# In-projection weights on another DMA queue, a table built in two steps, and gate weights issued after other tiles

## The chip, the cores and the metric

The kernel runs on one core of one Trainium2 chip. The metric is device time in microseconds (us), from the start of the launch on the core to its end; three runs of the kernel before gave 1465.84, 1471.44 and 1471.6 us.

## The reference

One layer of a hybrid decoder for 2048 positions and 1024 channels, all in float32. Cut to its steps:

```
h  = rmsnorm(x, norm_w)
u, zs, q, k, v, za = split(h @ w_in)             # 1024 -> 6 x 512 columns
ya = s5(u)                                       # 32 groups of 16 channels, complex state of 64,
                                                 #   scan over positions, gelu, half-GLU
ya = ya * silu(zs)
yb = differential_attention(rope(rmsnorm(q)), rope(rmsnorm(k)), v)   # 4 heads, two causal
                                                 #   softmax maps each, w1 - lambda * w2
yb = rmsnorm(yb) * 0.8 * silu(za)
x1 = x + concat(ya, yb) @ w_out                  # 1024 -> 1024
out = x1 + sigmoid(x1 @ w_gate) * (p @ w_proj)   # w_gate 1024 x 1024, w_proj 256 x 1024
```

## The kernel before

Every product is made from three TensorE products of rounded halves (high x high, high x low, low x high), so each operand exists as a pair: a cast on ScalarE (ACT) makes the high half, a subtraction on VectorE (DVE) or GpSimd (POOL) the low half. The program is written as Python generators, and a scheduler of the framework simulates a timeline and puts the instructions of each engine in one fixed order; each engine then runs its own list strictly in that order, DMA starts included. DMAs are started by SyncE (SP), a few by ACT.

**In-projection (0 to about 684 us).** It runs over 12 blocks, each 512 columns of `w_in` for one half of the positions, in the order u, u, k, zs, v, q, za, zs, k, v, q, za. A block has 8 weight chunks of 128 x 512. `build_w` (L276) makes one chunk: raw values into one of three `wraw` buffers (L279), `wh` on ACT (L282), `wl` on DVE (L283); `wh` and `wl` have 8 slots, one block's worth. So at the change from one block to the next the first three chunks already lie in `wraw`; their casts wait until the last tile of the old block has read the slots, and the raw loads of chunks 3 to 7 each wait until a `wl` has freed a `wraw` buffer. TensorE's products are at L757 (first block), L778 (u and zs) and L824 (q, k, v, za).

Between them runs the generator `ssm()`: for each quad of four channel groups `four()` (L546) builds parameter tables, among them the rotation table of each pair of groups (two products and a sum on DVE, L581 to L585) which goes out to `tab_scr` (L586) and comes back per group as `tab` (L599). `tx`, the tile that leaves, has one buffer, so the second pair's table waits until the first one has been stored. Then per group two products (L530), a rotation, a scan and a rotation back (L633 to L644).

**Attention (684 to about 1140 us).** Four heads, with the first half of the out-projection (L928) as filler.

**Second half of the out-projection (1140 to about 1235 us).** Eight tiles t of 256 positions. Tiles 0 to 2 (`EOP = 3`) run through a single PSUM tile `pmf`: each of their eight pieces is added to `x1` on DVE (L1185), and the next piece starts when that add is done. Tiles from 3 on use seven banks `pm3`, with one add for two pieces (L1189).

Beside it `gate_w()` (L1139) prepares the gate weights as seven sums of quadrants, four rounds k of two units each. A round loads two `wgr` tiles (two buffers in all, so a round's loads wait for the readers of the round before), gated by a one-column copy of the last finished `x1` (L1160, POOL); the units then make casts on ACT (L1149), differences (L1154) and low halves (L1150) on DVE and POOL. `GWS` says how many units are issued after which tile t, so it sets which `x1` a round's loads wait for: the one of the tile before.

**Gate product and per-layer input (1250 us to the end).** The operands are cast by ACT (`oph`, L1235); their pool lies where the `wgr`, `wgt` and `yin` buffers were, so the first cast waits for the last reader of those. L1262 is the gate product, L1278 the projection of p.

Of the kernel before, what the change touches and what calls it, by code (L numbers as in the profile page):

```python
# [11 lines left out]
F32 = mybir.dt.float32  # L12
# [3 lines left out]
ALU = mybir.AluOpType  # L16
# [49 lines left out]
WB = 8  # L66
ACB = 3
EOP = 3
GWS = {3: 2, 4: 2, 5: 3, 6: 1}
XEB = 14  # L70
RA3 = 2
SSE = 0
# [46 lines left out]
def hymba_kernel(ctx, tc, x_t, p_t, positions, norm_w, w_in, lam_re, lam_im, log_dt, b_re, b_im,  # L119
                 c_re, c_im, ssm_d, glu_w, glu_b, q_norm_w, k_norm_w, lq1, lk1, lq2, lk2,  # L120
                 subln_w, w_out, w_proj, w_gate, out):
    nc = tc.nc
    V, A, G, T = nc.vector, nc.scalar, nc.gpsimd, nc.tensor
    UE = (G, V)[SSE]
    win = w_in[0]
# [10 lines left out]
    tab_scr = [tc.dram_tile([128, 2, 17, 16], F32, name=f"tab_scr{i}") for i in range(16)]  # L136
# [61 lines left out]
    with ExitStack() as p1:  # L198
# [77 lines left out]
        def build_w(c0, k):  # L276
            def make():
                raw = pr.tile([128, 512], F32, name="wraw", bufs=WRB)
                nc.sync.dma_start(raw, win[k * 128:(k + 1) * 128, c0:c0 + 512])  # L279
                wh = pw.tile([128, 512], F32R, name="wh")  # L280
                wl = pw.tile([128, 512], F32R, name="wl")
                A.activation(wh, raw, AF.Copy, scale=nw[:, k:k + 1])  # L282
                V.scalar_tensor_tensor(wl, raw, nw[:, k:k + 1], wh.bitcast(F32), op0=ALU.mult, op1=ALU.subtract)  # L283
                return wh, wl
            return make
# [27 lines left out]
        def ssm():  # L313
# [55 lines left out]
            with tc.tile_pool(name="ssA", bufs=1) as sp:  # L369
                t32 = {}  # L370

                def nt(nm, shape=(128, NG)):
                    t32[nm] = sp.tile(list(shape), F32, name="s_" + nm)
                    return t32[nm]
# [7 lines left out]
                t1 = nt("t1")  # L382
# [38 lines left out]
                k = 1  # L421
# [8 lines left out]
                nr, den, t1 = nt("nr"), nt("den"), nt("t2")  # L430
# [46 lines left out]
                for (Tt, n_) in ((Tb, 16), (Ta, 16)):  # L477
                    V.memset(Tt[0][:, :, 0:1], 1.0)
                    V.memset(Tt[1][:, :, 0:1], 0.0)
                    k = 1  # L480
# [31 lines left out]
            with tc.tile_pool(name="ssB", bufs=2) as sp:  # L512
# [3 lines left out]
                def split(x_, nm, cols):  # L516

                    hi = sp.tile([128, cols], F32R, name=nm + "h", bufs=SPB[nm])
                    lo = sp.tile([128, cols], F32R, name=nm + "l", bufs=SPB[nm])
                    h_, l_ = hi, lo  # L520
                    if len(x_.shape) > 2:
                        g_, k_, p_ = x_.shape[1:]
                        h_, l_ = (t_.rearrange("q (g l p) -> q g l p", g=g_, l=k_) for t_ in (hi, lo))
                    A.copy(h_, x_)
                    V.tensor_tensor(l_, x_, h_.bitcast(F32), op=ALU.subtract)
                    return hi, lo
# [7 lines left out]
                def spread(par4, o_, l0):  # L534

                    r_ = sp.tile(sh, F32, name="na", bufs=1)
                    t_ = sp.tile([128, 2, 17, 16], F32, name="tabt", bufs=1).rearrange("q s a b -> q (s a b)")[:, :512]
                    t_ = t_.rearrange("q (g l p) -> q g l p", g=4, l=L)
                    V.tensor_tensor(r_, par4[:, :, o_:o_ + 16].unsqueeze(2).to_broadcast(sh),
                                    par4[:, :, 65 + l0:73 + l0].unsqueeze(3).to_broadcast(sh), op=ALU.mult)  # L540
                    V.tensor_tensor(t_, par4[:, :, o_ + 16:o_ + 32].unsqueeze(2).to_broadcast(sh),
                                    par4[:, :, 74 + l0:82 + l0].unsqueeze(3).to_broadcast(sh), op=ALU.mult)
                    V.tensor_tensor(r_, r_, t_, op=ALU.add)
                    return r_

                def four(q4, out_):  # L546


                    par4 = sp.tile([128, 4, NPAR], F32, name="parg")
                    nc.sync.dma_start(par4, par_scr[q4])  # L550
                    pt2 = sp.tile([128, 2, NTAB], F32, name="pt2", bufs=1)
                    nc.sync.dma_start(pt2, ptab_scr[q4])
                    na = spread(par4, 0, 1)

                    dd = sp.tile([128, 4, GP], F32, name="dd")
                    nc.sync.dma_start(dd.rearrange("q g p -> q (g p)"), ssm_d[0, q4 * 64:q4 * 64 + 64].partition_broadcast(128))
                    G.affine_select(out=dd, in_=dd, pattern=[[0, 4], [-1, GP]], compare_op=ALU.is_equal,
                                    fill=0.0, base=-112, channel_multiplier=1)
                    yield
                    pr_ = ps_ss.tile([128, 512], F32, name="pss")  # L560
                    for g in range(4):
                        T.matmul(pr_[:, g * 16:g * 16 + 16], lhsT=na[:, g].rearrange("q l p -> q (l p)"),
                                 rhs=par4[:, g, 32:48], start=True, stop=True)
                    rs = sp.tile([128, 64], F32, name="rs", bufs=1)
                    V.tensor_tensor(rs, pr_[:, :64], dd.rearrange("q g p -> q (g p)"), op=ALU.add)
                    nc.sync.dma_start(r_scr[q4][0:128, :], rs)
                    M = sp.tile([128, L, 64], F32, name="M", bufs=1)

                    r0 = r_scr[q4][0:128, :]
                    nc.sync.dma_start(M, bass.AP(tensor=r0.tensor, offset=r0.offset, ap=[[64, 128], [GP * 64, L], [1, 64]]))  # L570
                    pw_ = ps_ss.tile([128, 512], F32, name="pss")
                    for g in range(4):
                        T.transpose(pw_[:, g * 128:g * 128 + 128], na[:, g].rearrange("q l p -> q (l p)"), ident)
                    wa = split(pw_, "wa", 512)
                    yield

                    sht = [128, 2, 17, 16]
                    for e in range(2):
                        tx = sp.tile(sht, F32, name="tx", bufs=1)
                        t1 = sp.tile(sht, F32, name="tabt", bufs=1)  # L580
                        V.tensor_tensor(tx, pt2[:, e, 0:17].unsqueeze(1).unsqueeze(3).to_broadcast(sht),  # L581
                                        pt2[:, e, 34:66].rearrange("q (s b) -> q s b", s=2).unsqueeze(2).to_broadcast(sht), op=ALU.mult)
                        V.tensor_tensor(t1, pt2[:, e, 17:34].unsqueeze(1).unsqueeze(3).to_broadcast(sht),
                                        pt2[:, e, 66:98].rearrange("q (s b) -> q s b", s=2).unsqueeze(2).to_broadcast(sht), op=ALU.mult)
                        V.tensor_tensor(tx, tx, t1, op=ALU.add)  # L585
                        nc.sync.dma_start(tab_scr[q4 * 2 + e], tx)  # L586
                    yield
                    wc = spread(par4, 32, 0)
                    out_[q4] = par4, wa, M, wc
                    yield  # L590
# [15 lines left out]
                for _ in four(0, made):  # L606
                    pass
# [4 lines left out]
                for g in range(NG):  # L612
                    gl = g % 4
                    gs = slice(gl * 128, gl * 128 + 128)
                    if gl == 0:
                        par4, wa4, _, wc_raw = made.pop(g // 4)
                        parts = four(g // 4 + 1, made) if g < NG - 4 else iter(())
# [48 lines left out]
            with tc.tile_pool(name="ssC", bufs=1) as pg:  # L666
# [5 lines left out]
                for k in range(4):  # L672
                    for e in range(2):
                        raw = pg.tile([128, 256], F32, name="gg", bufs=GLB)
# [5 lines left out]
                for cq in range(8):  # L680
                    while ("zs", cq // 4) not in written:
                        yield
                    c0 = cq * 32
# [250 lines left out]
    with ExitStack() as p2:  # L934
# [90 lines left out]
        for h in range(H):  # L1025
# [6 lines left out]
            for i in ORD[h]:  # L1032
# [6 lines left out]
                for qt in range(2):  # L1039
# [16 lines left out]
                    c0 = 0  # L1056
# [67 lines left out]
    with ExitStack() as p3:  # L1124
# [12 lines left out]
        with ExitStack() as p3a:  # L1137
# [38 lines left out]
            for t, i in enumerate(order):  # L1176
# [15 lines left out]
                else:  # L1192
                    kept.append(x1)
                for _ in range(GWS.get(t, 0)):
                    next(gw)
# [200 lines left out]
```

## Time and profile before

| | |
|---|---|
| three runs | 1465.84, 1471.44, 1471.6 us (median 1471.44) |
| profiled execution | 1468.54 us, of it the span of the profile 1466.8 us |
| TensorE (PE) busy | 1389.2 us, 95% of the span |
| DVE, ACT, POOL busy | 73%, 52%, 36% |
| mean granted TensorE clock | 0.982 of full speed |

TensorE is busy nearly all the time, so a change can shorten the span by what TensorE waits (some 78 us in the whole program) and by the stretches that it runs at the lower clock behind a wait. Where it waits, and for whom, is in the rows further down. "[4.66 <-X]" behind a row says that the engine sat idle 4.66 us before it and that X ended the wait.

### The profile page before, as it was taken

To read this page: it belongs to the slowest core of one execution; us is meant where nothing else is said; L and a number is where in the kernel's file an instruction comes from. 1 tells how busy PE (TensorE), PEld (TensorE's weight loads), DVE (VectorE), ACT (ScalarE), POOL (GpSimd) and SP (SyncE) were. 2 spreads that over 40 slices of the span, in tenths; PEclk is the share of its full clock that TensorE was granted. 3 is DMA by queue.
4 is the path that set the end of the run, shared out by engine and by line. 5 is a ranking of instruction groups with operands and counts; after the bars stand their busy time and mean duration, and the time that the engine had idled before them with its cause. 6 is when DMAs were issued, how large, how long until landed. Compare 5 with 4: busy or idle time off the path is not lost.

```text
span 1466.8 us, 27419 instructions
## 1 busy us (share of the span) xinstructions
PE 1389.2 (95%) x9602; PEld 1279.5 (87%) x9602; DVE 1067.0 (73%) x2527; ACT 768.0 (52%) x1689; POOL 522.4 (36%) x670
## 2 busy tenths in 40 slices
PE   7999899999899999999899999999999996999998
PEld 7998798778698878888699999988989896899998
DVE  8568788789898866774687767767887248656754
ACT  8543335456554545553577677777787213332231
POOL 6632410043010411340255455544335334543440
PEclk9999899999999999999999999999999998899999
DMA  7448666546755287556854644644443455132221
GB/s 244 131 127 263 200 190 210 159 125 211 237 179 177 94 232 185 150 168 203 255 145 125 181 127 119 177 127 152 116 144 122 153 189 205 58 116 76 70 80 58
DMA packets 219410, 230.34 MB, mean 157 GB/s; under 512 B 62712, under 2 KB 168328, under 8 KB 216712
## 3 DMA queue, kind: packets, MB, share of 16 engines
q1 hardware_dynamic: 216968, 224.40, 49.8%
q10 hardware_dynamic: 2304, 4.20, 0.8%
q8 instruction: 75, 1.23, 0.3%
q14 instruction: 63, 0.52, 0.1%
HBM read 152.19 MB, written 84.72 MB: 162 GB/s over the span
## 4 chain that ended last, share of the span: by engine, by line
PE 48%; DVE 19%; DMA 15%; ACT 6%; issue 6%; POOL 5%; SPq 2%; ACTq 0%; DVEq 0%; POOLq 0%
PE pg L1262 11%; PE pmf L928 7%; PE po L1099 7%; PE pss L1063 7%; PE ptw L1095 3%; PE pl L1278 3%; DMA wraw<-in_w_in_dram 3%; PE pmm L824 2%; PE pss L707 2%; PE pmm L778 2%; POOL qst L846 2%; DMA tab_scr<-tx 2%; DVE wl L283 2%; PE pm L928 2%; DVE zz L644 1%
## 5 line engine op out<-in xcount | busy, mean ns | idle before, releaser
L824 PE MATMUL pmm<-wh,xh 128*128 128x512 f32 x512 | 197.6, 395 | 7.0 <-ACT wh L282 6.6
L824 PE MATMUL pmm<-wl,xh 128*128 128x512 f32 x512 | 200.8, 395 | 2.1 <-DVE wl L283 2.1
L824 PE MATMUL pmm<-wh,xl 128*128 128x512 f32 x512 | 200.2, 393 | 0.0
L1063 PE MATMUL pss<-ks,qd 128*128 128x512 f32 (+3 forms) x640 | 185.1, 387 | 7.5 <-DVE st L1065 4.0
L1074 ACT ACTIVATE s<-s,st 128x1024 f32<-128x1024 f32 (+4 forms) x192 | 171.5, 897 | 37.3 <-DVE st L1065 32.8
L1262 PE MATMUL pg<-oph,wg 128*128 128x256 f32 x896 | 164.1, 286 | 15.4 <-ACT oph L1235 15.4
L1262 PEld LDWEIGHTS pg<-oph,wg 128*128 128x128 f32 x896 | 141.6, 195 | 15.6 <-ACT oph L1235 15.6
L1099 PE MATMUL po<-vt,wt 128*128 128x128 f32 x1088 | 152.3, 276 | 2.9 <-ACT yo L1111 1.5
L1099 PEld LDWEIGHTS po<-vt,wt 128*128 128x128 f32 x1088 | 142.2, 192 | 11.2 <-ACT wt L1097 3.2
L1065 DVE CUSTOM_DVE_ANT_0 s<-pss,mk,st 128x512 f32<-128x512 f32 (+2 forms) x192 | 122.1, 651 | 23.3 <-PE pss L1063 21.7
L778 PE MATMUL pmm<-xh,wl 128*128 128x256 f32 x448 | 128.9, 291 | 4.1 <-DVE wl L283 4.1
L778 PE MATMUL pmm<-xh,wh 128*128 128x256 f32 x448 | 124.9, 294 | 6.0 <-DVE stg L788 3.2
L778 PE MATMUL pmm<-xl,wh 128*128 128x256 f32 x448 | 128.5, 290 | 0.0
L1262 PE MATMUL pg<-opl,wg 128*128 128x256 f32 x448 | 127.2, 285 | 0.3 <-POOL opl L1236 0.3
L824 PEld LDWEIGHTS pmm<-wh,xh 128*128 128x128 f32 x512 | 96.2, 189 | 27.6 <-ACT wh L282 8.7
L1063 PEld LDWEIGHTS pss<-ks,qd 128*128 128x128 f32 x640 | 100.8, 192 | 17.5 <-DVE st L1065 8.0
L824 PEld LDWEIGHTS pmm<-wl,xh 128*128 128x128 f32 x512 | 96.6, 189 | 21.1 <-DVE wl L283 3.0
L824 PEld LDWEIGHTS pmm<-wh,xl 128*128 128x128 f32 x512 | 96.7, 189 | 18.2
L928 PE MATMUL pmf<-yh,woh 128*128 128x256 f32 x352 | 105.0, 298 | 4.5 <-DVE x L1185 3.6
L596 POOL TENSOR_TENSOR U<-U,rl 128x256 f32<-128x256 f32 x32 | 28.3, 884 | 220.5 <-DMA U<-ug_scr 169.5
L1065 DVE CUSTOM_DVE_ANT_0 s<-pss,mk 128x512 f32<-128x512 f32 (+3 forms) x128 | 78.5, 629 | 31.2 <-PE pss L1063 26.7
L928 PE MATMUL pmf<-yl,woh 128*128 128x256 f32 x352 | 99.8, 284 | 0.0
(385 smaller groups left out, 3906.1 us busy)
## 6 DMA issues: line engine op xcount, KB each, us to landing
wraw<-in_w_in_dram SPq DMA_DIRECT2D x96, 256.0 KB
xraw<-in_x_t_dram SPq DMA_DIRECT2D x40, 256.0 KB
tab<-tab_scr SPq DMA_DIRECT2D x64, 136.0 KB
qd<-qh_scr SPq DMA_DIRECT2D x64, 128.0 KB
qd<-ql_scr SPq DMA_DIRECT2D x64, 128.0 KB
xr<-in_x_t_dram SPq DMA_DIRECT2D x32, 256.0 KB
yin<-yt_scr SPq DMA_DIRECT2D x16, 512.0 KB
xp_scr<-xp SPq DMA_DIRECT2D x32, 256.0 KB
```

The source lines that it names most:

```text
L283: V.scalar_tensor_tensor(wl, raw, nw[:, k:k + 1], wh.bitcast(F32), op0=ALU.mult, op1=ALU.subtract)
L707: T.matmul(pm[:, e, :], lhsT=a_[:, k, m * 128:m * 128 + 128], rhs=b_[k], start=(k == 0 and n == 0), stop=(k == 3 and n == 2))
L778: T.matmul(pm, lhsT=w[b_][:, cb * 128:cb * 128 + 128], rhs=xt[a_][:, k, :], start=(k == 0 and n == 0), stop=(k == 7 and n == 2))
L824: T.matmul(pm, lhsT=xt[a_][:, k, j * 128:j * 128 + 128], rhs=w[b_], start=(k == 0 and n == 0), stop=(k == 7 and n == 2))
L928: T.matmul(pm[:, e, :], lhsT=w[k][b_][:, ms], rhs=y[a_][:, k, :], start=(k == 0 and n == 0), stop=(k == 3 and n == 2))
L1063: T.matmul(pss[:, :cl], lhsT=qd[:, e, m, tq], rhs=ks[m][:, c0:c0 + cl], start=e == 0, stop=e == 1)
L1065: V.tensor_tensor_reduce(sr[m][pi][:, o:o + cl], pss[:, :cl], mk[:, end - cl:end], scale=1.0, scalar=3.4e38 if ci == 0 else st[:, 2 * ci - ...
L1074: A.activation(sr[m][pi][:, :cl], sr[m][pi][:, :cl], AF.Exp, bias=st[:, ci + m:ci + m + 1], scale=-1.0, accum_out=st[:, 12 + 2 * pi + m:13 ...
L1095: T.transpose(ptw[:, k, :], blocks_[kg + k], ident)
L1099: T.matmul(po[:, 0:128], lhsT=wt[:, k, :], rhs=vt[:, kg + k, :], start=kg + k == 0, stop=kg + k == len(blocks_) - 1)
L1262: T.matmul(banks[mp][:, e], lhsT=wg[n][k][b_][:, m * 128:m * 128 + 128], rhs=x_[a_][:, k], start=k == 0 and q == 0, stop=k == 3 and q == 2)
L1278: T.matmul(banks[mp][:, e], lhsT=wp[k][b_][:, m * 128:m * 128 + 128], rhs=p_[a_][:, k], start=(k == 0 and q == 0), stop=(k == 1 and q == 2))
```

## The change

Three edits. The raw chunks of `w_in` are started by ACT instead of SP. The rotation tables of a quad, built so far one after the other in one step of the generator, are built one ahead of the step's end and one in the next step. The gate weights' units are issued after tiles 2, 3, 4, 5 (two each) instead of 3, 4, 5, 6 (2, 2, 3, 1). Behind L556 all lines shift, from L592 on by three.

```diff
-GWS = {3: 2, 4: 2, 5: 3, 6: 1}
+GWS = {2: 2, 3: 2, 4: 2, 5: 2}
...
                 raw = pr.tile([128, 512], F32, name="wraw", bufs=WRB)
-                nc.sync.dma_start(raw, win[k * 128:(k + 1) * 128, c0:c0 + 512])
+                nc.scalar.dma_start(raw, win[k * 128:(k + 1) * 128, c0:c0 + 512])
...
+                    def table(e):
+                        ...                      # the loop's body from below, unchanged
...
                     wa = split(pw_, "wa", 512)
+                    table(0)
                     yield
-                    sht = [128, 2, 17, 16]
-                    for e in range(2):
-                        ...
-                        V.tensor_tensor(tx, tx, t1, op=ALU.add)
-                        nc.sync.dma_start(tab_scr[q4 * 2 + e], tx)
+                    table(1)
                     yield
```

On SP before, at the change to the ninth block (k of the second half), the raw chunks 3, 4 and 5 (`wraw_6356`, `wraw_6368`, `wraw_6380`) stand behind stores and loads of the background generator and of the zs block:

```order
L653 DMA yg_scr_60<-ysb_5327 128x256
L586 DMA tab_scr14_99<-tx_5494 128x544
L599 DMA tab_5509<-tab_scr13_98 64x544
L566 DMA r_scr7_68<-rs_5356 128x64
L599 DMA tab_5509<-tab_scr13_98 64x544
L808 DMA zs_scr_101<-t2_6157 128x2x256
L570 DMA M_5359<-r_scr7_68 128x8x64
L798 DMA zs_scr_101<-t2_6301 128x256
L279 DMA wraw_6356<-in_w_in_dram 128x512
L798 DMA zs_scr_101<-t2_6310 128x256
L279 DMA wraw_6368<-in_w_in_dram 128x512
L279 DMA wraw_6380<-in_w_in_dram 128x512
```

On ACT now, at the same place, they stand between the casts (`wh`), and the third of them and the fourth behind casts that wait for chunks 3 and 4 themselves:

```order
L524 CAST Uh_5723<-U_5717 128x256
L799 ACTIVATE t2_6310<-t2_6308 128x256
L282 ACTIVATE wh_6346<-wraw_6344,nw_186 128x512
L279 DMA wraw_6356<-in_w_in_dram 128x512
L279 DMA wraw_6368<-in_w_in_dram 128x512
L282 ACTIVATE wh_6358<-wraw_6356,nw_186 128x512
L524 CAST xah_5496<-md_5489 128x256
L637 COPY sw_5640<-pss_5626 64x256
L638 ACTIVATE sw_5640<-pss_5626 64x256
L279 DMA wraw_6380<-in_w_in_dram 128x512
L282 ACTIVATE wh_6370<-wraw_6368,nw_186 128x512
L799 ACTIVATE t2_6403<-t2_6401 128x256
```

The loads have left SP's list for ACT's. On DVE before, in the second half of the out-projection, the adds of tile 2 (`x1_14915`) and tile 3 (`x1_15028`) alternate:

```order
L1185 TENSOR_TENSOR x1_14915<-x1_14915,pmf_8818 128x256 x2
L1189 TENSOR_TENSOR x1_15028<-x1_15028,pm3_15036 128x512
L1185 TENSOR_TENSOR x1_14915<-x1_14915,pmf_8818 128x256
L1189 TENSOR_TENSOR x1_15028<-x1_15028,pm3_15062 128x512
L1185 TENSOR_TENSOR x1_14915<-x1_14915,pmf_8818 128x256
L1189 TENSOR_TENSOR x1_15028<-x1_15028,pm3_15088 128x512
L1185 TENSOR_TENSOR x1_14915<-x1_14915,pmf_8818 128x256
```

On DVE now, the first round of the gate weights stands among them (tile 3's sum is `x1_15056` here):

```order
L1188 TENSOR_TENSOR x1_14915<-x1_14915,pmf_8818 128x256 x2
L1157 TENSOR_TENSOR wgt_15036<-wgr_15028 128x512
L1192 TENSOR_TENSOR x1_15056<-x1_15056,pm3_15064 128x512
L1153 TENSOR_TENSOR wg33_14651<-wgt_15036,wg32_14650 128x512
L1157 TENSOR_TENSOR wgt_15040<-wgr_15029,wgt_15036 128x512
L1188 TENSOR_TENSOR x1_14915<-x1_14915,pmf_8818 128x256
L1157 TENSOR_TENSOR wgt_15046<-wgr_15029,wgt_15040 128x512
L1157 TENSOR_TENSOR wgt_15050<-wgr_15029,wgr_15028 128x512
L1153 TENSOR_TENSOR wg41_14665<-wgt_15040,wg40_14664 128x512
L1192 TENSOR_TENSOR x1_15056<-x1_15056,pm3_15090 128x512
L1153 TENSOR_TENSOR wg25_14643<-wgt_15046,wg24_14642 128x512
L1153 TENSOR_TENSOR wg49_14673<-wgt_15050,wg48_14672 128x512
```

Of the eight DVE instructions that a round of two units has, three now stand between the second and the third of tile 2's eight adds, and five between the third and the fourth; the fourth round now stands where the third was.

## Rows read from the trace of the kernel before

**Rows 1.** Windows by stage: length, busy of each engine, granted clock, DMA share, GB/s
```profile
0.00:684.00 684.00, 645.98 (x3907) 573.04 (x3907) 539.40 (x1350) 347.30 (x731) 190.50 (x224) 0.98 0.60 183
...
1140.00:1252.00 112.00, 93.08 (x753) 91.00 (x752) 58.50 (x80) 30.79 (x58) 42.96 (x43) 0.94 0.49 180
```
**Rows 2.** Timeline around the out-projection's end: start us, us, engine, line, operation
```profile
1234.39 0.28 PE L928 MATMUL pm<-yl,woh 128*128 128x256 f32 x1
1234.54 1.28 DVE L1150 TENSOR_TENSOR wg<-wgt,wg 128x512 fp32r<-128x512 f32 x2
...
1247.56 1.28 DVE L1150 TENSOR_TENSOR wg<-wgt,wg 128x512 fp32r<-128x512 f32 x2
1248.93 1.99 ACT L1235 CAST oph<-x 128x1024 fp32r<-128x1024 f32 x2 [2.98 <-DVE wg L1150]
...
1250.03 1.22 PE L1262 MATMUL pg<-oph,wg 128*128 128x256 f32 x4 [15.36 <-ACT oph L1235]
```
**Rows 3.** Windows behind that wait, columns as in rows 1
```profile
1250.00:1256.00 6.00, 5.67 (x24) 5.36 (x25) 2.90 (x1) 2.39 (x3) 5.95 (x3) 0.50 0.00 0
1256.00:1262.00 6.00, 6.00 (x52) 6.00 (x51) 0.69 (x1) 1.19 (x3) 1.57 (x1) 1.00 0.29 90
```
**Rows 4.** Timeline of SP: the loads of the gate weights
```profile
1193.21 1.34 SPq L1161 DMA_DIRECT2D wgr<-in_ple_w_gate_dram  x2
...
1221.59 13.31 SPq L1161 DMA_DIRECT2D wgr<-in_ple_w_gate_dram  x4
```
**Rows 5.** Timeline of DVE: tile 1's last add, tile 2's fifth, first gate round
```profile
1164.83 0.42 DVE L1185 TENSOR_TENSOR x<-x,pmf 128x256 f32<-128x256 f32 x1 [1.78 <-PE pmf L928]
...
1182.39 0.42 DVE L1185 TENSOR_TENSOR x<-x,pmf 128x256 f32<-128x256 f32 x1 [1.47 <-PE pmf L928]
...
1199.15 0.69 DVE L1154 TENSOR_TENSOR wgt<-wgr 128x512 f32<-128x512 f32 x1 [0.95 <-DMA wgr<-in_ple_w_gate_dram]
...
1201.59 4.59 DVE L1154 TENSOR_TENSOR wgt<-wgr,wgt 128x512 f32<-128x512 f32 x2
...
1207.80 1.89 DVE L1150 TENSOR_TENSOR wg<-wgt,wg 128x512 fp32r<-128x512 f32 x3
```
**Rows 6.** Timeline of POOL beside it
```profile
1203.89 3.44 POOL L1150 TENSOR_TENSOR wg<-wgr,wg 128x512 fp32r<-128x512 f32 x2
```
**Rows 7.** The page, part 5: in-projection groups, idle before them and its releaser
```profile
L824 PE MATMUL pmm<-wh,xh 128*128 128x512 f32 x512 | 197.6, 395 | 7.0 <-ACT wh L282 6.6
L824 PE MATMUL pmm<-wl,xh 128*128 128x512 f32 x512 | 200.8, 395 | 2.1 <-DVE wl L283 2.1
...
L778 PE MATMUL pmm<-xh,wl 128*128 128x256 f32 x448 | 128.9, 291 | 4.1 <-DVE wl L283 4.1
```
**Rows 8.** Timeline at the change to the ninth block
```profile
454.94 0.74 DVE L283 SCALAR_TENSOR_TENSOR wl<-wraw,nw,wh 128x512 fp32r<-128x512 f32 x1
...
461.99 0.38 SPq L279 DMA_DIRECT2D wraw<-in_w_in_dram  x1
...
468.28 0.72 ACT L282 ACTIVATE wh<-wraw,nw 128x512 fp32r<-128x512 f32 x1 [4.66 <-DMA wraw<-in_w_in_dram]
...
469.06 0.97 PE L824 MATMUL pmm<-wh,xh 128*128 128x512 f32 x3 [3.49 <-ACT wh L282]
```
**Rows 9.** Timeline at the change to the sixth block
```profile
285.69 0.73 DVE L581 TENSOR_TENSOR tx<-pt 128x544 f32<-128x544 f32 x1 [5.77 <-DMA tab_scr<-tx]
...
287.13 0.50 PE L824 MATMUL pmm<-wl,xh 128*128 128x512 f32 x1 [1.92 <-DVE wl L283]
...
294.63 0.73 PE L824 MATMUL pmm<-wh,xh 128*128 128x512 f32 x2 [1.17 <-ACT wh L282]
```
**Rows 10.** The tile tx: who waited for its store, us and times
```profile
  DVE tx L581: 14.0, 7
```
**Rows 11.** The DMA starts that ACT already makes: ns min/median/max
```profile
L839 ACTq DMA_DIRECT2D za_scr<-t x16: 326/326/386, 365.1 to 718.0; - x16
```
**Rows 12.** The tile wraw: its loads on SP; ns min/median/max, first and last start
```profile
L279 SPq DMA_DIRECT2D wraw<-in_w_in_dram x96: 327/334/1440, 1.7 to 660.4; - x96
```

More of the change, by code (lines that the diff above doesn't have):

```diff
@@ L552, in four @@
                     nc.sync.dma_start(pt2, ptab_scr[q4])
+                    def table(e):
+                        sht = [128, 2, 17, 16]
+                        tx = sp.tile(sht, F32, name="tx", bufs=1)
+                        t1 = sp.tile(sht, F32, name="tabt", bufs=1)
+                        V.tensor_tensor(tx, pt2[:, e, 0:17].unsqueeze(1).unsqueeze(3).to_broadcast(sht),
+                                        pt2[:, e, 34:66].rearrange("q (s b) -> q s b", s=2).unsqueeze(2).to_broadcast(sht), op=ALU.mult)
+                        V.tensor_tensor(t1, pt2[:, e, 17:34].unsqueeze(1).unsqueeze(3).to_broadcast(sht),
+                                        pt2[:, e, 66:98].rearrange("q (s b) -> q s b", s=2).unsqueeze(2).to_broadcast(sht), op=ALU.mult)
+                        V.tensor_tensor(tx, tx, t1, op=ALU.add)
+                        nc.sync.dma_start(tab_scr[q4 * 2 + e], tx)
                     na = spread(par4, 0, 1)
@@ L574, in four @@
                     wa = split(pw_, "wa", 512)
+                    table(0)
                     yield
-                    sht = [128, 2, 17, 16]
-                    for e in range(2):
[L579 to L584, printed above, removed]
-                        V.tensor_tensor(tx, tx, t1, op=ALU.add)
-                        nc.sync.dma_start(tab_scr[q4 * 2 + e], tx)
+                    table(1)
                     yield
```

## The prediction, made before the changed kernel ran

> **What bounds the kernel now.** I read the windows by stage first: the reader is to compare TensorE's busy time with the length of each stage. It waits 38.0 us of the first 684 and 18.9 us of the 112 from 1140 to 1252 [rows 1], so TensorE sets the pace, and a change gains only where one of these waits goes or a clock dip behind one. Then the timeline at the largest single wait: TensorE ends the out-projection at 1234.39 + 0.28 = 1234.67 us and starts the gate product at 1250.03. The row says 15.36 us idle, released by ACT's cast `oph`; that cast had waited for DVE's last gate low half, which ends at 1247.56 + 1.28 = 1248.84 [rows 2]. Behind it the granted clock is 0.50 (the 1.2 GHz level) for 6 us, in which 24 matmuls run, where 52 run in the next 6 us at 1.00 [rows 3]; the dip costs about 6 − 24 / 52 × 6 = 3.2 us. Last, the in-projection by the page's costliest groups: what TensorE waits for weight halves is 6.6 + 2.1 + 4.1 = 12.8 us [rows 7]; no move of the raw loads gains much more there than that and the dips behind it.
>
> **Gate weights.** The work stays the same, four rounds; only what each round waits for moves by one tile. Before, round 1 loads at 1193.21 behind tile 2, and rounds 3 and 4 at 1221.59 and about 1234 [rows 4] (the row of four holds both pairs). Now round 1 waits for tile 1, whose last add ends at 1164.83 + 0.42 = 1165.25 [rows 5], and rounds 2 to 4 take the places of 1 to 3. Round 3's last DVE instruction ended at 1234.54 + 1.28 = 1235.82 [rows 2], so that becomes the end of all rounds. The cast follows its release by 0.09 us and TensorE the cast by 1.10 us (1248.84, 1248.93, 1250.03 [rows 2]): gate product at about 1237.0 instead of 1250.03, −13.0 us. The wait left is 2.3 us; of the 3.2 us dip I take back 1.3, since a short wait may dip as well (bounds 0 and 3.2).
>
> Against it stands round 1 in its new place. Tile 2's adds come one by one, and TensorE's next piece through `pmf` waits for each. DVE's order puts eight gate instructions ahead of the fourth add. The first of them needs the load: 1193.21 to 1199.15 was 5.94 us, so with some 0.35 us for the copy and the start 1165.6 + 5.9 = 1171.5. From there to the end of the round took 1207.80 + 1.89 − 1199.15 = 10.5 us [rows 5], one L1189 add included; with one more of these (0.69) and the third `pmf` add (0.42) DVE is at 1171.5 + 11.6 = 1183.1, the fourth add ends at 1183.5, and the fifth starts one period of 1.78 + 0.42 = 2.20 us after the fourth's start, at 1185.3. Before, it started at 1182.39 [rows 5]. So tile 2 and all behind it are 2.9 us later. Bounds: 0 if the differences take 0.69 us each, as the first one does, and 5.5 if the loads land 2.6 us later beside the attention's last loads. TensorE waits there where it did not, and I add 1.7 us for half a dip (bounds 0 and 3.2).
>
> The long stretch in that round is two differences in 4.59 us instead of 2 × 0.69, and POOL's subtractions of the same tiles, 1.72 us each, run beside it [rows 5, 6]. The Trainium skill ("SBUF — State Buffer", Who interferes with whom) makes VectorE's second port pair one with GpSimd's, held by one of them for a whole instruction; the trace agrees as far as 4.59 against 1.38 goes. By that rule round 1 is as long in its new place, and the term is 2.9; without it, it would be about 0.
>
> Stage sum: −13.0 − 1.3 + 2.9 + 1.7 = −9.7 us; bounds −16 and −4.
>
> **Raw weights on ACT's queue.** 96 starts leave SP, and 96 × 0.33 = 32 us of starts come to ACT [rows 11, 12], which is busy 347 of 684 us there [rows 1]; no sum of its work makes ACT the bound, its order may. What goes is the wait behind SP's list. At the ninth block the `wraw` buffer is free at 454.94 + 0.74 = 455.68, the start comes at 461.99 (6.3 us later), the cast at 468.28, and TensorE has waited 3.49 us at 469.06 [rows 8]; SP was held by the stores and table loads that the order shows. With the load ahead by more than TensorE's wait, the whole wait goes: −3.6 with ACT's 0.1. At the sixth block TensorE waits 1.92 us for `wl`, DVE being held for 5.77 us by `tx`, whose store had not landed [rows 9]; a second wait of 1.17 us follows at 294.63 [rows 9], for a cast whose load was started late on SP too: −3.1 for both edits together. First load: SP starts it at 1.7 us [rows 12], behind two others, ACT can at once: −0.8 (bounds −1.7 and 0).
>
> The Trainium skill ("DMA: Bandwidth & Descriptors", Issuing engines are not separate DMA queues) says that starting DMAs from several engines saves only the starting time on the sequencer, usually small. The trace differs in one point: 6.3 us at the ninth block are no single start but a list of them and their waits. By the rule taken plainly, the move would give back 0.33 us at a place, nothing that counts.
>
> What is added is ACT's order. A start there stands in line with casts that wait: at five block changes the start of chunk 5 or of chunk 4 now comes behind the cast of chunk 3, which waits for that chunk's landing. Load to cast took 468.28 − 461.99 = 6.3 us and the cast 0.72 [rows 8], 7.0 in all; before, the next starts followed within about 1.5 us, and TensorE has some 1.4 us of products in chunks 3 and 4. So a change costs between 0, if the background's products cover it, and 7.0 − 1.5 − 1.4 = 4.1: 0 to 21 us for five. I take 3, near the lower end, since most chunks already go one by one and TensorE's whole wait for weights in 12 blocks is 12.8 us [rows 7].
>
> **Tables.** DVE's wait for the store of the first table is 14.0 us in seven places [rows 10]. With a step between them it goes, but DVE is not the bound; beyond the sixth block I count −1.3 us, one place where a product's operand stood behind it (bounds −4 and 0; a new stand of the first table ahead of a weight half could cost 1 to 2).
>
> In-projection: −0.8 − 3.6 − 3.1 − 1.3 + 3 = −5.8 us; bounds about −15 (all weight waits and a dip) and +13. Attention: no edit there; its order shifts a little and I take 0 (±3).
>
> **Sum.** −9.7 − 5.8 = −15.5: 1468.54 − 15.5 = 1453.0 us for the profiled execution (span 1466.8 and 1.7 around it). The median of the runs is 2.9 us above that execution, the lowest 2.7 below; I place the forecast 1 us up, 1454.
>
> **Rivals.** (1) The gate round pays and nothing else does: stage 1's gains (8.8) are eaten by ACT's order, or its waits move to the next chunk. Then 1468.5 − 9.7 + 1 = 1460, and up to 1463 with the stall of tile 2 at its bound. For it: most `wraw` starts were never late, and 0.33 us is all that a start costs. Against: 6.3 us in [rows 8].
>
> (2) The other side: ACT's list becomes the ring's bound. At each of the five changes the loads go strictly one after the other and half of the 7.0 us is not covered: +17.5, no gain in stage 1: 1468.5 − 9.7 + 17.5 = 1476, and by the median 1479. It decides from 9.7 / 5 = 1.9 us per change on. For it: three of five starts stand behind waiting casts in the new order. Against: ACT is idle half of the stage, and TensorE has the old block's tail and the background's products at each change.
>
> (3) Better: most of the 12.8 us and two dips of 3 us go, and the order's cost is 0: 1468.5 − 9.7 − 15 = 1444.
>
> **How the numbers follow.** Runs of this kernel tell a difference from none at about 0.5%, 7.4 us: faster is below 1464.1, slower above 1478.8. Forecast 0.58 (its own range 1447 to 1459), rival 1 0.20, rival 2 0.11, rival 3 0.11. Of these the forecast and rival 3 are faster, but for 0.06 of the forecast's tail, and half of rival 1 with its scatter: 0.58 − 0.06 + 0.11 + 0.10 = 0.73. Slower is rival 2 for the most part, 0.09. The rest, 0.18, is the same. The range 1443 to 1470 takes in the forecast, rival 1 and nearly all of rival 3.
>
> **What would show it.** The gate product starting within about 3 us of the last out-projection matmul, and its clock. Round 1's loads at about 1166 and a wait of TensorE for the fourth add of tile 2 of about 3 us. No TensorE wait of 3.5 us at the ninth block; ACT's wait for `wraw` at the chunks whose start stands behind a cast, and whether TensorE waits behind it. No DVE wait at `tx`. Wrong would be: round 4 ending as late as before because a round got longer; the in-projection ending later than 684 us; attention differing by more than 3 us.

## The result and the profile after

| | median us (from, to) | ratio to the kernel before, 95% interval |
|---|---|---|
| kernel before | 1469.65 (1465.84 to 1471.6) | |
| changed kernel | 1454.32 (1451.3 to 1456.38) | 0.9898 (0.9873 to 0.9923) |
| kernel before, beside other kernels later | 1468.42 (1461.19 to 1475.24) | |
| changed kernel, beside the same (e10) | 1454.98 (1452.43 to 1461.35) | 0.9926 (0.9905 to 0.9947) |

By these ratios the change makes the kernel 11 to 15 us faster, and the time is the one forecast. The profiled execution has a span of 1449.6 us against 1466.8. The windows of the changed kernel, by stage (length, busy time of each engine, granted clock, DMA share, GB/s):

```profile
0.00:684.00 684.00, 644.96 (x3930) 569.47 (x3930) 538.74 (x1351) 347.98 (x733) 193.08 (x224) 1.00 0.62 184
1140.00:1252.00 112.00, 105.92 (x850) 103.80 (x849) 69.86 (x86) 36.72 (x69) 54.44 (x51) 0.97 0.50 184
```

TensorE's busy time up to 684 us is what it was [rows 1]; most of the gain is in the second window, which holds 850 matmuls instead of 753. The first holds 3930 instead of 3907 at a granted clock of 1.00 instead of 0.98; in a second profile of the same kernel (e10) it holds 3902, so these 23 are no lasting gain. The timeline at the out-projection's end:

```profile
1228.23 0.28 PE L931 MATMUL pm<-yl,woh 128*128 128x256 f32 x1
1228.85 1.28 DVE L1153 TENSOR_TENSOR wg<-wgt,wg 128x512 fp32r<-128x512 f32 x2
...
1230.30 2.00 ACT L1238 CAST oph<-x 128x1024 fp32r<-128x1024 f32 x2 [1.92 <-DVE wg L1153]
1231.43 2.14 PE L1265 MATMUL pg<-oph,wg 128*128 128x256 f32 x8 [2.92 <-ACT oph L1238]
1234.73 0.58 PE L1265 MATMUL pg<-opl,wg 128*128 128x256 f32 x1 [1.16 <-POOL opl L1239]
```

The chain is the same as in [rows 2], DVE's last low half, ACT's cast, TensorE, but the 15.36 us are 2.92 (4.15 in the second profile, e10). Behind it there is a wait that hardly showed before (0.3 us for it on the page): 1.16 us for the first operand's low half on POOL. The windows from there on show that the dip to the lower clock stays:

```profile
1231.40:1237.40 6.00, 4.77 (x20) 4.21 (x21) 5.97 (x3) 2.46 (x3) 5.98 (x2) 0.53 0.00 0
1237.40:1243.40 6.00, 6.00 (x48) 6.00 (x47) 1.83 (x2) 2.23 (x4) 3.44 (x3) 0.90 0.12 44
```

20 and 48 matmuls in 12 us, where [rows 3] have 24 and 52: nothing came back of the dip. SP's timeline and DVE's show the first gate round in its new place:

```profile
1159.07 0.42 SPq L1164 DMA_DIRECT2D wgr<-in_ple_w_gate_dram  x1
...
1160.56 0.90 SPq L1164 DMA_DIRECT2D wgr<-in_ple_w_gate_dram  x1
...
1187.05 1.35 SPq L1164 DMA_DIRECT2D wgr<-in_ple_w_gate_dram  x2
```
```profile
1158.25 0.42 DVE L1188 TENSOR_TENSOR x<-x,pmf 128x256 f32<-128x256 f32 x1 [0.47 <-PE pmf L931]
...
1165.42 0.69 DVE L1157 TENSOR_TENSOR wgt<-wgr 128x512 f32<-128x512 f32 x1 [2.13 <-DMA wgr<-in_ple_w_gate_dram]
...
1168.30 0.68 DVE L1157 TENSOR_TENSOR wgt<-wgr,wgt 128x512 f32<-128x512 f32 x1
1168.90 0.41 DVE L1188 TENSOR_TENSOR x<-x,pmf 128x256 f32<-128x256 f32 x1
1169.23 1.50 DVE L1157 TENSOR_TENSOR wgt<-wgr,wgt 128x512 f32<-128x512 f32 x1
1170.65 1.78 DVE L1157 TENSOR_TENSOR wgt<-wgr 128x512 f32<-128x512 f32 x1
...
1174.76 0.41 DVE L1188 TENSOR_TENSOR x<-x,pmf 128x256 f32<-128x256 f32 x1
1176.95 0.42 DVE L1188 TENSOR_TENSOR x<-x,pmf 128x256 f32<-128x256 f32 x1 [1.19 <-PE pmf L931]
```

The first L1188 row is tile 1's last add; it ends at 1158.67, and the round's loads start at 1159.07 and 1160.56. The other three are tile 2's third, fourth and fifth add by their place between the gate instructions: the fourth starts 9.34 us after the round's first instruction, and the fifth 2.19 us later. In the in-projection, the two groups that answer to [rows 7], and the tile `tx` for [rows 10]:

```profile
L827 PE MATMUL pmm<-wh,xh 128*128 128x512 f32 x512 | 198.3, 396 | 3.9 <-ACT wh L282 2.8
...
L781 PE MATMUL pmm<-xh,wl 128*128 128x256 f32 x448 | 127.2, 287 | 2.7 <-DVE wl L283 2.6
```
```profile
  DVE tx L558: 15.8, 5
```

The waits for weights fell from 12.8 to 5.4 us, the wait for the table's store did not fall (14.0). What TensorE waits for now (engine, tile, line, whom it waits for: us in total, times, longest):

```profile
PE pmm L760 <- ACT xh L223: 6.1, 1, 6.1
...
PE pss L530 <- ACT ysb L655: 3.2, 3, 2.6
PE pss L530 <- DVE wal L525: 3.1, 1, 3.1
PE pss L530 <- DVE xal L525: 2.9, 6, 0.8
```

The background's products (L530) wait now. The change to the ninth block shows it in small:

```profile
455.33 0.39 PE L530 MATMUL pss<-Uh,wah 128*128 128x256 f32 x1 [2.60 <-ACT ysb L655]
...
458.98 0.33 ACTq L279 DMA_DIRECT2D wraw<-in_w_in_dram  x1
...
460.45 0.40 PE L827 MATMUL pmm<-wh,xh 128*128 128x512 f32 x1
...
462.09 0.72 ACT L282 ACTIVATE wh<-wraw,nw 128x512 fp32r<-128x512 f32 x1 [2.19 <-DMA wraw<-in_w_in_dram]
```

Load to cast is 3.11 us, not 6.3 [rows 8], and the buffer was free only 0.03 us before the start; the 3.49 us of waiting for `wh` are gone, and 2.60 us of waiting stand ahead of a background product, 5.12 us before the block's first product at 460.45. In the kernel before, the same product (the first of the 29th of 32 groups of L530) stood behind the block's first product and waited for nothing:

```profile
458.96 0.39 PE L824 MATMUL pmm<-wh,xh 128*128 128x512 f32 x1
...
472.39 0.28 PE L530 MATMUL pss<-Uh,wah 128*128 128x256 f32 x1
```

So TensorE's order has changed too, and not only the queue of the loads.

To compare kernels stage by stage I use one number: what TensorE has lost up to a time, which is that time minus the matmuls started by then at full rate (start to start 110 ns for 128 columns, 120 for 256, 227 for 512, medians of the kernel before; 1346.2 us in all).

| profiled kernel | lost by 684 us | by 1155 us | from there to the end |
|---|---|---|---|
| before | 63.4 | 92.0 | 28.6 |
| gate edit alone (e1) | 60.9 | 89.0 | 17.5 |
| table edit alone (e3) | 63.8 | 91.2 | 29.0 |
| ACT's queue alone (e2) | 62.0 | 89.8 | 28.5 |
| changed kernel | 58.4 | 87.8 | 15.6 |
| changed kernel again (e10) | 64.5 | 90.0 | 17.9 |
| no weight loads (e9) | 49.7 | 89.4 | 27.3 |
| best, loads on ACT (e8) / on SP (e11) | 59.5 / 61.8 | 88.7 / 91.8 | 12.0 / 12.4 |

The last column separates the kernels; the first two scatter between executions of one and the same list. By 684 us the changed kernel has lost 58.4 and, again, 64.5; before and e1, whose traces have TensorE's matmuls in the same order until 1176 us, differ by 2.5. By 1155 us such pairs differ by 2 to 3 us.

### The profile page after: what moved, and what is told of

Read it like the earlier page. It is cut to its first block, busy times and chain, and to the rows that moved or that the text cites. A ratio compares the mean times of both kernels' runs of the same rounds, so it can differ in the third digit from the quotient of the medians.

```text
span 1449.6 us, 27391 instructions
## 1 busy us (share of the span) xinstructions
PE 1383.4 (95%) x9602; PEld 1270.7 (88%) x9602; DVE 1066.3 (74%) x2527; ACT 767.9 (53%) x1689; POOL 521.3 (36%) x670
## 4 chain that ended last, share of the span: by engine, by line
PE 37%; DVE 5%; ACT 3%; issue 2%; DMA 2%; POOL 1%; SPq 0%; DVEq 0%; ACTq 0%; POOLq 0%
PE pg L1265 11%; PE po L1102 7%; PE pmf L931 6%; PE pss L1066 6%; PE pl L1281 3%; PE ptw L1098 3%; ACT s L1077 2%; DVE wgt L1157 1%; DVE s L1068 1%; PE pm L931 1%; DVE s L1090 1%; DMA wgr<-in_ple_w_gate_dram 1%; DVE wg L1153 0%; DMA yt_scr<-yo 0%; DMA yin<-yt_scr 0%
## 5 line engine op out<-in xcount | busy, mean ns | idle before, releaser
L827 PE MATMUL pmm<-wh,xh 128*128 128x512 f32 x512 | 198.3, 396 | 3.9 <-ACT wh L282 2.8
L827 PE MATMUL pmm<-wl,xh 128*128 128x512 f32 x512 | 200.4, 395 | 0.0
L827 PE MATMUL pmm<-wh,xl 128*128 128x512 f32 x512 | 200.0, 393 | 0.0
L1066 PEld LDWEIGHTS pss<-ks,qd 128*128 128x128 f32 x640 | 100.4, 192 | 22.8 <-DVE st L1068 11.6
L827 PEld LDWEIGHTS pmm<-wh,xh 128*128 128x128 f32 x512 | 96.1, 188 | 25.3 <-ACT wh L282 5.7
L827 PEld LDWEIGHTS pmm<-wl,xh 128*128 128x128 f32 x512 | 96.5, 188 | 19.2 <-DVE wl L283 1.5
L827 PEld LDWEIGHTS pmm<-wh,xl 128*128 128x128 f32 x512 | 96.5, 189 | 18.6
L1068 DVE CUSTOM_DVE_ANT_0 s<-pss,mk 128x512 f32<-128x512 f32 (+3 forms) x128 | 78.6, 630 | 34.3 <-PE pss L1066 28.6
L931 PE MATMUL pmf<-yh,wol 128*128 128x256 f32 x352 | 99.8, 284 | 0.0
```

The source lines that it names most:

```text
L827: T.matmul(pm, lhsT=xt[a_][:, k, j * 128:j * 128 + 128], rhs=w[b_], start=(k == 0 and n == 0), stop=(k == 7 and n == 2))
L931: T.matmul(pm[:, e, :], lhsT=w[k][b_][:, ms], rhs=y[a_][:, k, :], start=(k == 0 and n == 0), stop=(k == 3 and n == 2))
L1066: T.matmul(pss[:, :cl], lhsT=qd[:, e, m, tq], rhs=ks[m][:, c0:c0 + cl], start=e == 0, stop=e == 1)
L1068: V.tensor_tensor_reduce(sr[m][pi][:, o:o + cl], pss[:, :cl], mk[:, end - cl:end], scale=1.0, scalar=3.4e38 if ci == 0 else st[:, 2 * ci - ...
```

## The experiments

**Each edit alone.** In the traces the gate edit leaves TensorE's order in the in-projection as it was, and the table edit leaves the order of all its 9602 matmuls (by tile, buffer numbers left out), so the three can be measured one by one.

```diff
-GWS = {3: 2, 4: 2, 5: 3, 6: 1}
+GWS = {2: 2, 3: 2, 4: 2, 5: 2}          # e1 alone
-    nc.sync.dma_start(raw, win[...])
+    nc.scalar.dma_start(raw, win[...])   # e2 alone
+    table(0); yield; table(1)            # e3 alone
```

> The kernel before with the gate rounds' edit alone (GWS 2,3,4,5). By the prediction's own sum: the gate product starts about 13.0 us earlier, tile 2 of the out-projection stalls about 2.9 us behind DVE's first round (fourth add at about 1183.5 instead of 1178.1), the clock dips give 1.3 back and take 1.7: in all -9.7 us, ratio 0.9934. Rival: the round finds its place in DVE's idle time without a stall, as in the changed kernel, then -12 to -14 us, ratio about 0.991. In-projection and attention as in the kernel before.

Measured: 0.9924 (0.9901 to 0.9947), 1457.32 us, −11.2 us of 1468. The rows of tile 2's stall and of the gate product, and TensorE's waits in the in-projection:

```profile
1173.48 0.39 PE L928 MATMUL pmf<-yh,woh 128*128 128x256 f32 x1 [0.56 <-DVE x L1185]
...
1234.16 0.71 PE L1262 MATMUL pg<-oph,wg 128*128 128x256 f32 x4 [2.57 <-ACT oph L1235]
```
```profile
PE pmm L824 <- ACT wh L282: 4.1, 4, 2.8
...
PE pss L530 <- DVE wal L525: 2.2, 1, 2.2
```

The gap closes as in the changed kernel. The stall of tile 2 is there, but start to start TensorE loses 0.7 us ahead of one piece and 0.3 ahead of the next, not 2.9. The interval (−14.5 to −7.8 us) holds both −9.7 and the rival's −12 to −14; the last column, −11.1, lies between.

> The kernel before with the raw weight loads on ACT's queue alone. By the prediction's sum: -0.8 at the start, -3.6 at the ninth block, some of -3.1 at the sixth, +3 for ACT's order, about -4.5 us, ratio 0.997; the end of the in-projection 4 to 5 us earlier, the gate gap of 15 us unchanged. Rival 1: the weight waits go but waits of the background's products take their place, and the total stays within 2 us (ratio 0.999 to 1.001). Rival 2: ACT's order is the ring's bound, the in-projection ends later than before (ratio over 1.002).

Measured: 0.9991 (0.9976 to 1.0005), 1467.33 us. TensorE's waits:

```profile
PE pss L530 <- ACT ysb L652: 3.4, 1, 3.4
PE pss L530 <- DVE wal L525: 3.0, 1, 3.0
...
PE pmm L824 <- ACT wh L282: 2.9, 4, 1.2
PE pss L530 <- ACT xah L524: 2.8, 3, 2.2
```

Rival 1. Over all rows of this view the waits for weight halves are 5.9 us where before had 15.2 and e1 11.2 (left out is the wait ahead of the very first matmul: 5.4 and 5.5 us for `wh` there, 5.7 for `xh` here; the 12.8 us of [rows 7] leave out 2.4 for `wh` at L778). The background products' waits (L530, with L573 in before and e1) are 13.5 where both had 5.7, and all waits together 36.6 against 37.2 and 36.2.

> The kernel before with the rotation tables' split alone. By the prediction's sum -1.3 us (ratio 0.999) and DVE's 14.0 us of waits for the store of tx gone. Rival: the written order of the two steps changes next to nothing in the lists of the engines, tx waits stay near 14 us and the total is the same within 1 us.

Measured: 1.0004 (0.9988 to 1.0019), 1468.97 us; the rival, with 15.4 us of waits for `tx` in five places:

```profile
  DVE tx L558: 15.4, 5
```

**One tile earlier still.**

```diff
-GWS = {2: 2, 3: 2, 4: 2, 5: 2}
+GWS = {1: 2, 2: 2, 3: 2, 4: 2}
```

> The changed kernel with the gate units issued after tiles 1, 2, 3, 4 instead of 2, 3, 4, 5. If the 2.9 us that TensorE still waits ahead of the gate product are the last round's end, the wait shrinks to about 1.5 to 2 us (DVE's last add and ACT's cast remain) and the total falls by about 1 us against the changed kernel, ratio to the kernel before about 0.989. Rival: the first round now falls into the attention's tail and costs there what it gives, or the first rounds stall tiles 1 and 2: 0 to 4 us slower than the changed kernel.

Measured: 0.9945 (0.9921 to 0.9968), 1461.25 us. The wait shrank as expected, the rest went as the rival has it: TensorE lost 1.6 us at 1152 and 2.1 us at 1184 in waits ahead of `pmf` pieces, so the total is no better than the changed kernel's (the intervals overlap).

```profile
1238.37 0.74 PE L1265 MATMUL pg<-oph,wg 128*128 128x256 f32 x4 [1.25 <-ACT oph L1238]
```

**Whose list is it?** Two tries at keeping the weights' gain without the products' waits: another queue, and the background's priority set back.

```diff
-    nc.scalar.dma_start(raw, win[...])
+    nc.gpsimd.dma_start(raw, win[...])   # e5
-LAG = 20
+LAG = 80                                 # e6
```

> The changed kernel with the raw weight loads on GpSimd's queue instead of ACT's. Seen so far: on ACT's queue alone the total moves by -0.9 in a thousand; TensorE's waits for weight halves fall from 17 to 21 us to about 6, its waits for the background's products (L530) rise from 6 to 12 or 13. If ACT's own list (starts standing between casts) is what takes the gain, this queue keeps the weight waits low and the product waits near 6, and the total is 3 to 6 us below the changed kernel (ratio to before about 0.987). If any move of the loads off SP's list lets the scheduler put the background's products earlier than their operands come, the product waits are 10 us or more here too and the total is as the changed kernel's (ratio 0.990 to 0.994).

Measured: 1.0155 (1.0136 to 1.0173), 1490.82 us: neither total. A start takes POOL 538 ns and POOL waits 74.6 us for the buffers to come free; the waits for weights, the first one included, are back at 20.2 us (20.6 before). The products' are at 10.4, though ACT starts no load here.

```profile
L279 POOL DMA_DIRECT2D wraw<-in_w_in_dram x96: 538/538/782, 1.3 to 677.7; - x96
```

> The changed kernel with the background's priority set back (LAG 80 instead of 20), which changes the order in the in-projection only. If the waits for the background's products (12 us) come from products that stand too early in TensorE's list, they fall to about 6 us here, the weight waits stay near 6, and the total is 3 to 6 us below the changed kernel. If they come from the products' own chain (cast, store and load of M, table), they stay at 10 us or more, or others of the same size take their place, and the total stays within 2 us of the changed kernel.

Measured: 0.997 (0.9951 to 0.9988), 1463.67 us, slower than the changed kernel. The products still wait 13.5 us in all:

```profile
PE pss L530 <- DVE wal L525: 3.0, 1, 3.0
...
PE pss L530 <- ACT xah L524: 2.8, 3, 2.1
PE pss L530 <- DVE xal L525: 2.5, 6, 0.8
```

But the edit did not move them. In the traces all 288 matmuls of L530 have the same places in TensorE's order as in the changed kernel; L710, L827 and L868 have other ones, nearly all from 520 us on. By the measure of the table above e6 has lost 57 us by 520 us (e10: 56) and 100 by 1155 (e10: 90), so it falls back where its order differs. Whether the products stand too early is therefore not tested. The traces speak for it: the first products of the 32 groups stand 14 to 105 places earlier (median 32) than in the kernel before in every kernel with the loads on ACT, with products' waits of 11.5 to 14.0 us, and 31 to 176 places earlier in e5. The kernels with the loads on SP (e1, e3, e7, e11) have the places of the kernel before, and waits of 5.7 to 7.1 us. No run moves the loads and keeps the places, so it is not shown whether the place or ACT's list makes these waits.

**What the loads can be worth at all.**

```diff
-    raw = pr.tile([128, 512], F32, name="wraw", bufs=WRB)
-    nc.sync.dma_start(raw, win[...])
+    if len(raws) < WRB:
+        raws.append(pc.tile([128, 512], F32, name=f"wraw{len(raws)}"))
+        nc.sync.dma_start(raws[-1], win[...])
+    raw = raws[k % len(raws)]
```

> The kernel before without 93 of the 96 raw loads of w_in: three chunks are loaded and every block casts from them, so no weight ever waits for a load (the result's weights are wrong, all arithmetic is done). If the loads' waits were a cost of their own, the in-projection ends 10 to 16 us earlier and the total falls by that (ratio about 0.991). If the in-projection is held by the background's chain and by ACT and DVE, so that other waits take the loads' place, the total falls by less than 4 us (ratio above 0.997), with TensorE's waits for the products (L530) at 10 us or more.

Measured: 0.9991 (0.9968 to 1.0015). The in-projection does get ahead, by 13.7 us at 684, and the attention gives it back. The first two windows of e9, then the second one of the kernel before:

```profile
0.00:684.00 684.00, 653.16 (x3971) 580.15 (x3972) 534.61 (x1362) 349.34 (x743) 197.89 (x228) 0.99 0.52 151
684.00:1140.00 456.00, 436.84 (x3178) 403.79 (x3177) 333.58 (x941) 328.08 (x805) 204.44 (x360) 0.98 0.51 144
```
```profile
684.00:1140.00 456.00, 441.74 (x3226) 407.46 (x3225) 337.69 (x956) 334.09 (x825) 206.57 (x368) 0.99 0.51 151
```

TensorE is busy 7.2 us more than before in the first window [rows 1] and 4.9 us less in the second. By 1155 us the kernel has lost 89.4 us, the changed one 87.8, before 92.0. So the expectation's second half was wrong on the place (the products' waits are 8.4 us), and right on the sum. Its attention has another list too, since the scheduler's timeline moved; whether the list or the attention's own chain gives the lead back stays open.

**DVE beside POOL, and a better version.**

```diff
-    made(1, r1[:, c1], G)
+    made(1, r1[:, c1], V)                # e7, likewise made(2, ...) and made(3, ...)
-    yield made(xi_[:, K1])
+    yield made(xi_[:, K1], V if first else G)   # e8 and e11: with e7's edit, first pair only
```

> The gate rounds' edit alone, and all low halves of the gate weights made on DVE instead of three in seven on POOL. If DVE's long differences (4.59 us for two, 1.78 for one, against 0.69) come from POOL's subtractions and casts of the same time, they fall to 0.7 us each wherever POOL does nothing, though DVE has 12 instructions more; a round's DVE stretch then is about 11 x 0.68 = 7.5 us beside 9 to 10.5. The load of the next round is not faster, so the gate gap stays 2 to 3 us. Rival: the long differences are waits for the second tile's load, then they stay.

Measured once, 1453.08 us. The same eight differences, first of e1, then of this kernel (busy us, mean ns, idle before):

```profile
L1154 DVE TENSOR_TENSOR wgt<-wgr,wgt 128x512 f32<-128x512 f32 x8 | 15.2, 1895 | 0.2
```
```profile
L1154 DVE TENSOR_TENSOR wgt<-wgr,wgt 128x512 f32<-128x512 f32 x8 | 5.5, 686 | 0.0
```

They fall to the length of an undisturbed one; the long ones were waits for POOL, not for a load. The gate gap did not stay at 2 to 3 us as expected:

```profile
1233.04 0.71 PE L1262 MATMUL pg<-oph,wg 128*128 128x256 f32 x4 [1.18 <-ACT oph L1235]
```

> The changed kernel with the gate weights' low halves on DVE and the first operand's low half of the gate product on DVE too (POOL's takes some 3 us there, and TensorE waits 1.2 to 1.8 us for it after the first products, part of it at the lower clock). Expected: that wait gone, the rounds a little shorter, 1 to 3 us below the changed kernel, ratio to before 0.988 to 0.991. Rival: DVE becomes the one waited for ahead of the gate product (its sums for the third and fourth operand come later) and nothing is won.

Measured: 0.9887 (0.987 to 0.9905), 1452.42 us. Both waits ahead of the gate product are shorter:

```profile
1230.32 0.71 PE L1265 MATMUL pg<-oph,wg 128*128 128x256 f32 x4 [1.18 <-ACT oph L1238]
...
1232.19 0.39 PE L1265 MATMUL pg<-opl,wg 128*128 128x256 f32 x1 [0.23 <-DVE opl L1239]
```

> The changed kernel once more, beside the two neighbours on the same chip: ratio 0.988 to 0.993; the three edits measured alone add up to 0.992 (0.9924, 0.9991, 1.0004).

Measured: 0.9926 (0.9905 to 0.9947), 1454.98 us, in line with the parts' 0.992.

> The version with the gate weights' low halves and the first operand's low half on DVE, with the raw loads back on SP's queue. If ACT's queue is worth its 1 us, this is about 1 us slower than with ACT's queue, ratio 0.988 to 0.991; if ACT's queue only moves waits, the two are the same within the interval.

Measured: 0.9887 (0.9864 to 0.9911), 1451.13 us. With the loads on SP or on ACT the two best versions have the same ratio, and both lose some 12 us behind 1155, 3 to 6 less than the changed kernel's 15.6 and 17.9. They beat the kernel before; against the changed kernel the intervals overlap.

## Why the prediction was right

**The gate rounds.** Right in mechanism and nearly in size. The gap went from 15.36 to 2.92 us (2.3 forecast; 2.57 in e1, 4.15 in e10), the loads came behind tile 1, the rounds took each other's places. The whole stage was put at −9.7; the column behind 1155 us gives −11.1 (e1 against before) and −10.6 and −12.9 (changed kernel against e2). Two terms were mis-sized. The stall of tile 2, +2.9, measured 1.0 in e1 and less than 0.6 at any piece of the changed kernel: I had taken the round's length from a round in which POOL also made a `yl` (2.41 us) between its subtractions, and in the new place that one had run before. From the first gate instruction to the fourth add it is 9.34 us, not 11.6; the two differences of 4.59 us took 0.68 and 1.50. And the dips, −1.3 and +1.7, did not go either way: no new dip beside tile 2 (granted clock 1.00 from 1158 to 1194 us, in e1 too), none given back at the gate product, where POOL's low half now makes TensorE wait a second time.

The rule of the Trainium skill ("SBUF — State Buffer", Who interferes with whom) on VectorE's second port pair holds here: 1.90 us with POOL at work on the same tiles, 0.69 without. How much of POOL's work falls beside has to be read for each place; that was the error in the term.

**The raw loads on ACT.** The waits that I named are gone: the start follows the free buffer at once, the waits of 3.49, 1.92 and 1.17 us for weights do not appear. But −4.5 us for it (−0.8, −3.6, −3.1, +3) is not there: −1.3 by e2, with an interval from −3.5 to +0.7. The step that failed is "the whole wait goes": it went from the weights to the products, which is the prediction's first rival, for this part alone. By the sum, the move cost about 6 us and not the 3 that I took (an estimate: 7.5 us of forecast gains less the 1.3 measured), and in another place than I looked: not at the next weight but at the background's products. I put that cost down to ACT's order; that is not shown, since the products also stand earlier in TensorE's order than before. The start came out wrong in sign: the load is started at 0.8 us, but ACT's cast of x now stands behind, and TensorE begins at 6.12 instead of 5.45 us. e9 fits: with no load to wait for the in-projection was 13.7 us ahead at 684 us and the total was the same. As its order is another one, in the attention too, it sets no bound on what the waits are worth.

The rule of the Trainium skill on issuing engines ("DMA: Bandwidth & Descriptors", Issuing engines are not separate DMA queues) gives the right total for this edit, next to nothing, though for another reason than the one it names: at the ninth block the start came 0.03 us after the buffer was free instead of 6.3.

**The tables.** −1.3 forecast, +0.6 measured with 2 us to either side. The wait for the store did not fall (14.0 us before, 15.4 in e3, 15.8 in the changed kernel): e3's trace has TensorE's matmuls and SP's transfers in the order of the kernel before. I had read the change in the code and not in the list.

**The total.** The parts alone sum to −11.9 us (−11.2, −1.3, +0.6), and the changed kernel was measured at −15.0 and −10.9, the forecast was −15.5. That the time itself is met within a microsecond owes something to chance. The in-projection's 5.1 us too many were made good in part by the gate's 1.5 too few; the other 3.6 lie within the scatter between the two measurements of the same kernel. The start of the sum was sound: 1468.54 and 1 us up, where the kernel before had 1469.65 beside the changed one.

## What to carry to other kernels

A wait in a view is worth what is left when the next operand in line is late too: where several chains feed one in-order engine, count the waits of all of them together, and see whether the sum falls. A wait at the border between two stages, with nothing else to run, was worth nearly its whole length here (e1: 12.8 us less of it, 11.2 us less in all); look there first. And when an instruction is priced from a row, look at what the neighbouring engine did in that row and whether it will do it in the new place. Where a scheduler sets the order, check in the trace that an edit moved what it was meant to move, and nothing else: e6 left its products in place, and the loads' new queue moved them.

## What was not expected of the hardware

Differences of two tiles in SBUF on DVE take 0.69 us alone and on average 1.90 us over e1's eight, with POOL's subtractions from the same tiles beside them (0.69 in e7, where DVE makes those). A DMA start costs 0.33 us on ACT and SP and 0.54 us on POOL here.
